# Mixer parameters first, eight halves of modulation weights beside each FFN, and the merge's weight splits on VectorE

## The chip, the cores and the metric

The kernel runs on one core of a Trainium2 chip. Its time is the device time of one execution in microseconds. The engines are named as in the profile: PE (TensorE), DVE (VectorE), ACT (ScalarE), POOL (GpSimd) and SP, the queue that issues nearly all DMAs. Each engine works through its own instruction stream in order and waits where an operand is not ready.

## The reference, cut to what matters

Two layers run over 384 tokens (128 context, 256 latent) of width 1024. Each layer is a macaron block:

```
x += 0.5 * g1 * SwiGLU1(mod(rms(x)))            # FFN 0 of the layer, inner width 2816
x += g2 * Mix(mod(rms(x)))                      # four mixers, sigmoid-gated merge, output projection
x += 0.5 * g3 * SwiGLU2(mod(rms(x)))            # FFN 1 of the layer
```

`mod` scales and shifts by modulation vectors. A layer has nine of them (mod 0 to 8); each is `cond @ w_ada[:, 1024*mod : 1024*mod+1024] + b` for two conditionings, one for context and one for latent tokens. The mixers are a gated DeltaNet (chunked, with a triangular solve), a differential attention with QK norm, rotary and a scalar lambda from `da_lambda`, an mLSTM, and a retention with learned decay. The merge computes `sum over m of sigmoid(h @ w_gate[m]) * (branch[m] @ w_branch[m])`. Everything is in float32.

## The kernel before, in words

A float32 product is made of three TensorE matmuls over operands that are split into a high and a low part (`mm3`, L185 to L187): high by high, high by low and low by high. Activations are split once. Weights are split as they arrive: SP loads a raw block of 1 MB (`raw`, three buffers), ACT casts it to `whi` (L168), and DVE or POOL subtracts, `wlo = raw - whi` (L172). `whi` and `wlo` have three buffers each. One such split of 128x1024 elements feeds 24 matmuls of 384 columns.

An FFN is a gate/up part and a down part. Gate/up takes 44 splits; after each pair comes a Silu on ACT, a product and a second split of the hidden activations (L578, L582 on DVE). The down part takes 22 splits in two groups of output columns; each group ends with residual additions into the state (`resid`, L538), squares for the next norm (L380) and POOL's scaling of the new state (L386).

Modulation vectors are computed beside the FFNs, in two ways. A job on TensorE (`ada`) loads half a weight block (`araw`, 2 x 1 MB), and runs 16 matmuls (`arow`, L261) and, once for a vector, four transposes (`acol`, L271). The way beside, `ada_beside`, does a half (512 columns) on DVE: it loads four `braw` blocks of 512 KB (two buffers), runs 16 accumulations of 128x512 (`acc`, L315 and L317), and two transposes with two reductions (L323, L324); eight tiny matmuls (L329) finish a vector. It is cut into steps of two instructions, ten for a half, and the FFN's `split` lets one step follow each weight split that DVE does. What is left when the splits are through runs at the end of the FFN.

In the mixers small parameter loads stand where they are used. In the attention mixer, SP loads `rope`, `bgn` and `blp` (the lambda vectors), DVE multiplies and reduces `blp` (L1112, L1113), and POOL builds `brg` from the norm gains and the rotary table (L1102, L1107). The DeltaNet solve is a forward substitution on DVE: 31 rows, each a product (L1335, growing from 112x1 to 112x961) and a reduction (L1337), one after the other. Beside it TensorE has the rest of the attention and work of the merge to do: gates (`mg`, one split and 24 matmuls each) and products (`pb`) with the branch weights, each finished by one DVE instruction on `y` (L1485). In the merge, the low parts of the splits for the mixers m = 3, 2 and 1 (the tuple POOLM: 24 gates and 6 branch halves a layer) are on POOL, and those of m = 0 on DVE.

The order of each engine's instructions is set when the kernel is built: a scheduler with a simulated timeline places instructions by its own costs, and what it wrote is then fixed.

Of the kernel before, what the change touches and what calls it, by code (L numbers as in the profile page):

```python
# [20 lines left out]
KD = 8  # L21
# [17 lines left out]


LOOK, NBR, LAG = 2, 8, 7
POOLM = (3, 2, 1)
EARLY = (10, 7)
EARLY0 = 6
RING, NT1, NT2 = 256 * 305, 6, 4
R_G, R_B, R_CV, R_NG, R_RT, R_N = 0, 24, 96, 114, 118, 122
# [70 lines left out]
class Trunk:  # L117
# [431 lines left out]
    def ffn_body(self, l, i, jobs, beside, nxt):  # L549
        nc, I = self.nc, self.I  # L550
        g = None
# [38 lines left out]
        for dg in range(2):  # L590
            acc = [self.mmps(name="pd") for _ in range(4)]
            units = []
            for f in range(0, KF, 4):
                nf = min(4, KF - f)
                raw = self.load_raw(
                    I["ffn_w_down"][l, i, 128 * f:128 * (f + nf), 512 * dg:512 * dg + 512].rearrange(
                        "(k p) n -> p k n", p=128), [128, nf, 512])
                for q in range(0, nf, 2):
                    w = split(raw[:, q:q + 2], [128, 2, 512])
                    units += [(f + q + r, w[0][:, r], w[1][:, r]) for r in range(2)]  # L600
                    if f + q < KF - 4:
# [113 lines left out]
    def gate_stage(self, l, keep, p):  # L715
        nc, I = self.nc, self.I
        grow = p.tile([128, T], F32, tag="grow", name="grow")
        nc.scalar.copy(grow, self.proj_gates(l))
        gb = p.tile([128, 4, 8], F32, tag="gb", name="gb")
        nc.vector.memset(gb[:, 0], 0.0)  # L720
        al = p.tile([128, 8], F32, tag="al", name="al")
        for dst, nm in ((gb[:, 1], "dn_dt_bias"), (gb[:, 2], "ml_i_bias"), (gb[:, 3], "ml_f_bias"), (al, "dn_a_log")):
            nc.sync.dma_start(dst, I[nm][l].rearrange("d h -> (d h)").unsqueeze(0).to_broadcast([128, 8]))
# [17 lines left out]
        nc.scalar.activation(out=al, in_=al, func=AF.Exp)  # L741
# [114 lines left out]

    def mix_ret(self, l, p):
        nc, I = self.nc, self.I
        lg = p.tile([128, 12], F32, name="lg")
        nc.sync.dma_start(lg[:, 0:8], I["ret_decay_logit"][l].rearrange("d h -> (d h)").unsqueeze(0).to_broadcast([128, 8]))  # L860
        nc.vector.tensor_copy(lg[:, 8:12], self.prm[l][:, R_RT:R_RT + 4])
        nc.vector.tensor_scalar_mul(lg, lg, -1.0)
        self.softplus(lg, [128, 12])
        nc.vector.tensor_scalar_mul(lg, lg, -1.0)
# [225 lines left out]

    def mix_attn(self, l, p):
        nc, I = self.nc, self.I
        lam0 = 0.8 - 0.6 * math.exp(-0.3 * l)
        rope = p.tile([128, 2, 2, 32], F32, name="rope")
        nc.sync.dma_start(rope, I["rope"])
        gn = p.tile([128, 2, 32], F32, name="bgn")
        nc.sync.dma_start(gn[:, 0], I["da_qn_g"][l:l + 1].to_broadcast([128, 32]))
        nc.sync.dma_start(gn[:, 1], I["da_kn_g"][l:l + 1].to_broadcast([128, 32]))

        rg = p.tile([128, 2, 2, 2, 32], F32, name="brg")  # L1100
        for b in range(2):
            nc.gpsimd.tensor_tensor(rg[:, b, 0], gn, rope[:, b, 0].unsqueeze(1).to_broadcast([128, 2, 32]), op=ALU.mult)  # L1102
            for a in range(2):
                sv, gv, ov = (t.rearrange("p i (g a e) -> p i g a e", a=2, e=8) for t in (
                    rope[:, b, 1].unsqueeze(1).to_broadcast([128, 2, 32]), gn, rg[:, b, 1]))
                for i in range(2):
                    nc.gpsimd.tensor_tensor(ov[:, i, :, a], gv[:, i, :, 1 - a], sv[:, i, :, a], op=ALU.mult)  # L1107
        lp = p.tmp([128, 2, 2, 32], "blp")
        nc.sync.dma_start(lp, I["da_lambda"][l].rearrange("a d -> (a d)").unsqueeze(0).to_broadcast([128, 128]).rearrange(
            "p (a b d) -> p a b d", a=2, b=2))  # L1110
        lam = p.tile([128, 2], F32, name="blam")
        nc.vector.tensor_tensor(lp[:, :, 0], lp[:, :, 0], lp[:, :, 1], op=ALU.mult)  # L1112
        nc.vector.tensor_reduce(lam, lp[:, :, 0], axis=AX, op=ALU.add)  # L1113
        nc.scalar.activation(out=lam, in_=lam, func=AF.Exp)
        nlam = p.tile([128, 1], F32, name="bnlam")
        nc.vector.scalar_tensor_tensor(nlam, lam[:, 1:2], -lam0, lam[:, 0:1], op0=ALU.add, op1=ALU.subtract)
        gcol = p.tile([128, 1], F32, name="bgc")
        nc.vector.tensor_scalar_mul(gcol, self.prm[l][:, R_NG + 1:R_NG + 2], 1.0 - lam0)
# [322 lines left out]
    def merge(self, l, br, y):  # L1441
# [2 lines left out]
        pend, cur = [], {}  # L1444

        def gate(m, d):
            eng = nc.gpsimd if m in POOLM else nc.vector
            if d % 2 == 0:
                cur["g"] = self.wcols(I["w_in"][l], C_MERGE + 1024 * m + 128 * d)
            q = d % 2  # L1450
            w = self.split_unit(cur["g"][:, :, 128 * q:128 * q + 128], [128, KD, 128], eng)
            ps = self.hidden(w, "mg")
            if m > 1 or d % 4 == 3:
                s = self.wp.tile([128, T], F32, tag="nt", name="mgs", bufs=2)
            else:
                s = self.bp.tile([128, T], F32, tag="br", name="mgs", bufs=NBR)
            with self.tc.high_priority():
                nc.scalar.activation(out=s, in_=ps, func=AF.Tanh, scale=0.5)
            pend.append((m, d, s))

        def prepare(m, d):
            eng = nc.gpsimd if m in POOLM else nc.vector
# [32 lines left out]
        for t in range(n):  # L1495
# [6 lines left out]
            for i, u in enumerate(due):  # L1502
# [62 lines left out]
    def run(self):  # L1565
        with self.es:
# [6 lines left out]
            for l in range(2):  # L1573
                if l:
                    self.norm()
                else:
                    with self.after(self.last_load):
                        self.nc.sync.dma_start(self.cst[:, NC1:], self.I["cst2"])
                mods = {(0, 0): (0, (2, 3, 4)), (0, 1): (0, (8,)), (1, 0): (1, (3, 4)), (1, 1): None}
                slow = {(0, 0): ((0, 5), (0, 6), (0, 7)), (0, 1): ((1, 0), (1, 1), (1, 2)), (1, 0): ((1, 5), (1, 6), (1, 7)),  # L1580
                        (1, 1): ((1, 8),)}
                jobs = [self.ada(mods[l, i][0], *mods[l, i][1]) if mods[l, i] else iter(()) for i in range(2)]
# [34 lines left out]
```

## Time and profile before

| | |
|---|---|
| time, median of 3 runs | 2138.11 us (2131.19 to 2139.86) |
| profiled execution | 2140.96 us, span 2139.2 us |
| mean granted TensorE clock | 0.978 |
| PE busy | 2062.1 us (96%) |
| DVE busy | 1469.3 us (69%) |
| ACT busy | 842.9 us (39%) |
| POOL busy | 466.2 us (22%) |
| read from device memory | 313.00 MB |

The stages lie in the trace at about: FFN 0 of layer 0 until 333 us, its mixers and merge until 830 us, FFN 1 until 1110 us, FFN 0 of layer 1 until 1385 us, its mixers and merge until 1870 us, and the last FFN. A time in a row is counted from the start of the span. "Idle before" is what an engine waited in front of an instruction, with what ended the wait.

### The profile page before, as it was taken

What the parts mean: (1) busy time and instruction counts of PE and PEld (TensorE: products, weight loads), DVE (VectorE), ACT (ScalarE), POOL (GpSimd) and SP (SyncE); (2) the same over time, 40 slices, a digit from 0 to 9 for tenths busy, and PEclk for the clock granted to TensorE, in tenths of its full rate; (3) what the DMA queues carried; (4) which work ended last, traced back from release to release, by engine and by line L of the source; (5) the groups of instructions that cost most, each with busy time, mean ns of one, the idle gap of its engine ahead of it and who ended that gap; (6) DMA issues with size and microseconds to landing.
All of it is one profiled execution on the core that took longest, in us unless ns stands there. A gap on an engine that the chain in (4) does not pass through costs nothing.

```text
span 2139.2 us, 31932 instructions
## 1 busy us (share of the span) xinstructions
PE 2062.1 (96%) x12450; PEld 1992.0 (93%) x12450; DVE 1469.3 (69%) x2716; ACT 842.9 (39%) x1514; POOL 466.2 (22%) x375
## 2 busy tenths in 40 slices
PE   7999999988899999999999999999888999999999
PEld 5889999888789999999999999999877999999999
DVE  4867678678955578776778776678699445795433
ACT  3533335453343245333344332363533423463322
POOL 3000014434354252000120000243243722500000
PEclk8999999999899999999999999999998999999999
DMA  9775545434142355565467554444332423454432
GB/s 312 266 266 171 172 139 173 132 97 121 52 123 70 111 187 171 185 186 178 148 221 260 169 177 168 144 127 138 99 99 77 116 72 129 148 167 128 135 123 79
DMA packets 280566, 322.75 MB, mean 151 GB/s; under 512 B 42784, under 2 KB 214368, under 8 KB 280160
## 3 DMA queue, kind: packets, MB, share of 16 engines
q1 hardware_dynamic: 280144, 320.46, 47.7%
q8 instruction: 98, 1.61, 0.3%
q14 instruction: 52, 0.43, 0.1%
q10 hardware_dynamic: 272, 0.26, 0.0%
HBM read 313.00 MB, written 7.69 MB: 150 GB/s over the span
## 4 chain that ended last, share of the span: by engine, by line
PE 83%; DVE 13%; DMA 2%; ACT 1%; issue 1%; SPq 0%; DVEq 0%; ACTq 0%
PE pg L185 6%; PE pd L185 6%; PE pg L186 6%; PE pd L186 6%; PE pd L187 6%; PE pg L187 6%; PE pu L187 6%; PE pu L185 6%; PE pu L186 6%; PE mg L187 3%; PE mg L185 3%; PE mg L186 3%; DVE aR L1335 2%; PE mm L185 1%; PE mm L186 1%; PE mx L1389 1%
## 5 line engine op out<-in xcount | busy, mean ns | idle before, releaser
L168 ACT CAST whi<-raw 128x1024 fp32r<-128x1024 f32 x422 | 442.6, 1050 | 880.8 <-PE pd L186 212.9
L172 DVE TENSOR_TENSOR wlo<-raw,whi 128x1024 fp32r<-128x1024 f32 x324 | 401.3, 1239 | 304.1 <-ACT whi L168 298.8
L172 POOL TENSOR_TENSOR wlo<-raw,whi 128x1024 fp32r<-128x1024 f32 x98 | 246.4, 2518 | 331.6 <-ACT whi L168 304.9
L386 POOL TENSOR_SCALAR xg<-xT,gs 128x128 f32<-128x128 f32 (+1 forms) x96 | 92.8, 982 | 798.3 <-DVE xT L538 775.7
L185 PE MATMUL pd<-hh,whi 128*128 128x384 f32 x704 | 237.6, 337 | 0.0
L186 PE MATMUL pd<-hl,whi 128*128 128x384 f32 x704 | 237.3, 337 | 0.0
L187 PE MATMUL pd<-hh,wlo 128*128 128x384 f32 x704 | 234.8, 337 | 0.0
L317 DVE SCALAR_TENSOR_TENSOR acc<-braw,cond,acc 128x512 f32<-128x512 f32 x280 | 198.7, 749 | 0.2 <-DMA braw<-in_w_ada 0.2
L185 PE MATMUL pg<-hhi,whi 128*128 128x384 f32 x536 | 180.2, 336 | 0.0
L186 PE MATMUL pg<-hlo,whi 128*128 128x384 f32 x536 | 179.4, 335 | 0.0
L187 PE MATMUL pg<-hhi,wlo 128*128 128x384 f32 x536 | 179.3, 334 | 0.0
L185 PE MATMUL pu<-hhi,whi 128*128 128x384 f32 x536 | 179.1, 334 | 0.0
L187 PE MATMUL pu<-hhi,wlo 128*128 128x384 f32 x536 | 179.1, 334 | 0.0
L186 PE MATMUL pu<-hlo,whi 128*128 128x384 f32 x536 | 179.1, 334 | 0.0
L185 PE MATMUL mg<-hhi,whi 128*128 128x384 f32 x512 | 178.0, 348 | 0.0
L186 PE MATMUL mg<-hlo,whi 128*128 128x384 f32 x512 | 177.3, 346 | 0.0
L187 PE MATMUL mg<-hhi,wlo 128*128 128x384 f32 x512 | 175.5, 344 | 0.9 <-DVE wlo L172 0.9
L186 PEld LDWEIGHTS pd<-hl,whi 128*128 128x128 f32 x704 | 132.3, 188 | 0.1
L185 PEld LDWEIGHTS pd<-hh,whi 128*128 128x128 f32 x704 | 132.3, 188 | 0.1
L187 PEld LDWEIGHTS pd<-hh,wlo 128*128 128x128 f32 x704 | 132.1, 188 | 0.0
L185 PEld LDWEIGHTS pg<-hhi,whi 128*128 128x128 f32 x536 | 100.6, 188 | 3.6 <-ACT hh L581 3.4
L186 PEld LDWEIGHTS pg<-hlo,whi 128*128 128x128 f32 x536 | 100.7, 188 | 1.7 <-issue 1.7
(417 smaller groups left out, 4629.5 us busy)
## 6 DMA issues: line engine op xcount, KB each, us to landing
raw<-in_w_in SPq DMA_DIRECT2D x62, 1024.0 KB
raw<-in_ffn_w_gate SPq DMA_DIRECT2D x44, 1024.0 KB
raw<-in_ffn_w_up SPq DMA_DIRECT2D x44, 1024.0 KB
braw<-in_w_ada SPq DMA_DIRECT2D x80, 512.0 KB
raw<-in_ffn_w_down SPq DMA_DIRECT2D x40, 1024.0 KB
araw<-in_w_ada SPq DMA_DIRECT2D x32, 1024.0 KB
raw<-in_w_branch SPq DMA_DIRECT2D x16, 512.0 KB
raw<-in_w_out SPq DMA_DIRECT2D x8, 1024.0 KB
```

What stands on the lines that cost most here:

```text
L168: nc.scalar.copy(hi, src)
L172: self.last_split = (eng or nc.vector).tensor_tensor(lo, src, hi.bitcast(F32), op=ALU.subtract)
L185: nc.tensor.matmul(ps, w[0], x[0], start=start, stop=False)
L186: nc.tensor.matmul(ps, w[0], x[1], start=False, stop=False)
L187: self.last_mm = nc.tensor.matmul(ps, w[1], x[0], start=False, stop=stop)
L317: nc.vector.scalar_tensor_tensor(acc[s], raw[:, g], c, acc[s], op0=ALU.mult, op1=ALU.add)
L386: self.nc.gpsimd.tensor_scalar(xg[kk][:, a:e], self.xT[:, kk, a:e], gs[:, s, kk:kk + 1], None, op0=ALU.mult)
L1335: nc.vector.tensor_tensor(pr, X[:, 0:r, 0:r].rearrange("p k c -> p c k"), M[:, r, 0:r].unsqueeze(1).to_broadcast([112, r, r]), op=ALU.mult)
L1389: nc.tensor.matmul(ps[:, 64 * h:64 * h + 64], Z[d][:, b, h], x[:, 64 * h:64 * h + 64], start=(h == 0), stop=(h == 3))
```

## The change

There are three parts. First, the parameter loads of the mixers and the small work on them move into `mixer_parameters`, which is written ahead of everything else in `mixers`. Second, in an FFN's down part two steps of `ada_beside` follow each split in place of one, and the vectors move: the TensorE jobs lose three (mod 4 of layer 0, mods 3 and 4 of layer 1), and the work beside grows from six halves to eight in three FFNs. Third, POOLM is gone: all gate and branch splits of the merge have their low part on DVE.

```
-POOLM = (3, 2, 1)
...
-        def split(src, shape):
+        def split(src, shape, n=1):
             w = self.split_unit(src, shape)
             if self.last_split.ins.engine == mybir.EngineType.DVE:
                 with self.after(self.last_split):
-                    next(beside, None)
+                    for _ in range(n):
+                        next(beside, None)
...
-                    w = split(raw[:, q:q + 2], [128, 2, 512])
+                    w = split(raw[:, q:q + 2], [128, 2, 512], 2)
...
         def gate(m, d):
-            eng = nc.gpsimd if m in POOLM else nc.vector
...
-            w = self.split_unit(cur["g"][:, :, 128 * q:128 * q + 128], [128, KD, 128], eng)
+            w = self.split_unit(cur["g"][:, :, 128 * q:128 * q + 128], [128, KD, 128])
...
-                cur["w"] = self.split_unit(cur["raw"].pop(0), [128, 2, 512], eng)
+                cur["w"] = self.split_unit(cur["raw"].pop(0), [128, 2, 512])
...
+    def mixer_parameters(self, l):
...
+        lp = self.ring.tmp([128, 2, 2, 32], "blp")
...
+        for dst, nm in ((self.gb[:, 1], "dn_dt_bias"), (self.gb[:, 2], "ml_i_bias"), (self.gb[:, 3], "ml_f_bias"),
+                        (self.al, "dn_a_log"), (self.lg[:, 0:8], "ret_decay_logit")):
+            nc.sync.dma_start(dst, I[nm][l].rearrange("d h -> (d h)").unsqueeze(0).to_broadcast([128, 8]))
+        nc.sync.dma_start(lp, I["da_lambda"][l].rearrange("a d -> (a d)").unsqueeze(0).to_broadcast([128, 128]).rearrange(
+            "p (a b d) -> p a b d", a=2, b=2))
...
     def mixers(self, l):
         nc = self.nc
         with self.pool("bp") as self.bp:
+            self.mixer_parameters(l)
...
-                mods = {(0, 0): (0, (2, 3, 4)), (0, 1): (0, (8,)), (1, 0): (1, (3, 4)), (1, 1): None}
-                slow = {(0, 0): ((0, 5), (0, 6), (0, 7)), (0, 1): ((1, 0), (1, 1), (1, 2)), (1, 0): ((1, 5), (1, 6), (1, 7)),
-                        (1, 1): ((1, 8),)}
+                mods = {(0, 0): (0, (2, 3)), (0, 1): (0, (8,))}
+                slow = {(0, 0): ((0, m) for m in (4, 5, 6, 7)), (0, 1): ((1, m) for m in (0, 1, 2, 3)),
+                        (1, 0): ((1, m) for m in (4, 5, 6, 7)), (1, 1): ((1, 8),)}
```

The rows below are instructions in the order that the builds give an engine, with the line, the operation, out<-in and the shape. The lines of the changed kernel are its own.

VectorE near the end of the down part of the first FFN, before (`wlo` is a weight split, `acc` the work beside, the memsets belong to the mixers):

```order
L172 TENSOR_TENSOR wlo<-raw,whi 128x1024
L317 SCALAR_TENSOR_TENSOR acc<-braw,cond,acc 128x512 x2
L720 MEMSET gb 128x8
L172 TENSOR_TENSOR wlo<-raw,whi 128x1024
L317 SCALAR_TENSOR_TENSOR acc<-braw,cond,acc 128x512 x2
L647 MEMSET raw 128x1024
L791 MEMSET mp 36x3
L784 MEMSET m_3220 36x1
L172 TENSOR_TENSOR wlo<-raw,whi 128x1024
L317 SCALAR_TENSOR_TENSOR acc<-braw,cond,acc 128x512 x2
```

The same place in the changed kernel:

```order
L171 TENSOR_TENSOR wlo<-raw,whi 128x1024
L316 SCALAR_TENSOR_TENSOR acc<-braw,cond,acc 128x512 x2
L171 TENSOR_TENSOR wlo<-raw,whi 128x1024
L316 SCALAR_TENSOR_TENSOR acc<-braw,cond,acc 128x512 x2
L800 COPY mp<-m_3307 4x1 x2
L316 SCALAR_TENSOR_TENSOR acc<-braw,cond,acc 128x512 x2
L171 TENSOR_TENSOR wlo<-raw,whi 128x1024
L316 SCALAR_TENSOR_TENSOR acc<-braw,cond,acc 128x512 x4
L322 STREAM_TRANSPOSE acct<-acc 128x512
L171 TENSOR_TENSOR wlo<-raw,whi 128x1024
```

Two accumulations follow a split before; now most splits have four behind them, and the work beside runs until the last split.

VectorE in the later half of the substitution of layer 0, before (`aR` is the substitution; `bmx`, `brc`, `bsum`, `be` the attention's softmax; `y` a product of the merge):

```order
L1335 TENSOR_TENSOR aR<-aR 112x529
L1184 TENSOR_SCALAR bmx<-bmx 128x2
L1337 TENSOR_REDUCE aR<-aR 112x23
L1335 TENSOR_TENSOR aR<-aR 112x576
L1193 RECIPROCAL brc<-bsum 128x2
L1337 TENSOR_REDUCE aR<-aR 112x24
L1194 SCALAR_TENSOR_TENSOR bsum<-brc,bnlam,bsum 128x1
L1335 TENSOR_TENSOR aR<-aR 112x625
L1195 SCALAR_TENSOR_TENSOR be<-be,bsum 128x384
L1337 TENSOR_REDUCE aR<-aR 112x25
L1335 TENSOR_TENSOR aR<-aR 112x676
L1485 SCALAR_TENSOR_TENSOR y<-mgs,pb 128x384
```

The same place in the changed kernel:

```order
L1300 TENSOR_TENSOR aR<-aR 112x484
L171 TENSOR_TENSOR wlo<-raw,whi 128x1024
L1448 SCALAR_TENSOR_TENSOR y<-mgs,pb 128x384
L1302 TENSOR_REDUCE aR<-aR 112x22
L1158 RECIPROCAL brc<-bsum 128x2
L1300 TENSOR_TENSOR aR<-aR 112x529
L1159 SCALAR_TENSOR_TENSOR bsum<-brc,blam,bsum 128x1
L1302 TENSOR_REDUCE aR<-aR 112x23
L1160 SCALAR_TENSOR_TENSOR be<-be,bsum 128x384
L1300 TENSOR_TENSOR aR<-aR 112x576
L171 TENSOR_TENSOR wlo<-raw,whi 128x1024
L1448 SCALAR_TENSOR_TENSOR y<-mgs,pb 128x384
```

The splits now stand between the rows of the substitution: 11 between its first and its last product, where there was none, and 10 merge products there in place of 7.

VectorE where `blp` was multiplied, in the attention mixer of layer 0, before (`fr` and `nu` are steps of an inverse square root, `co` an output of the retention or mLSTM):

```order
L161 SCALAR_TENSOR_TENSOR fr<-nu,fr 128x12
L159 SCALAR_TENSOR_TENSOR nu<-fr 128x12
L160 TENSOR_TENSOR nu<-nu,nv 128x12
L1112 TENSOR_TENSOR blp<-blp 128x2x32
L161 SCALAR_TENSOR_TENSOR fr<-nu,fr 128x12
L666 TENSOR_TENSOR co<-co,fr 128x256 x3
L172 TENSOR_TENSOR wlo<-raw,whi 128x1024
```

Where it stands in the changed kernel, at the start of the first FFN of layer 0:

```order
L171 TENSOR_TENSOR wlo<-raw,whi 128x1024
L316 SCALAR_TENSOR_TENSOR acc<-braw,cond,acc 128x512 x2
L578 TENSOR_TENSOR sg<-sg,hn 128x384 x2
L271 TENSOR_REDUCE sb<-acol 128x4
L1497 TENSOR_TENSOR blp<-blp 128x2x32
L209 TENSOR_TENSOR hn<-pg,sqacc 128x384
L209 TENSOR_TENSOR hn<-pu,sqacc 128x384
L582 TENSOR_TENSOR hl<-sg,hh 128x384 x2
```

The scheduler moved the layer 0 instance ahead of the mixers by a whole FFN, with its load right behind the load of a raw gate block; that of layer 1 went into the merge of layer 0.

## Rows read from the trace of the kernel before

**Rows 1.** The page: busy time by engine, and the chain that ended last by engine.

```profile
PE 2062.1 (96%) x12450; PEld 1992.0 (93%) x12450; DVE 1469.3 (69%) x2716; ACT 842.9 (39%) x1514; POOL 466.2 (22%) x375
...
PE 83%; DVE 13%; DMA 2%; ACT 1%; issue 1%; SPq 0%; DVEq 0%; ACTq 0%
```

**Rows 2.** Windows: us, busy (instructions) of five engines, PE clock, DMA share, GB/s.

```profile
100.00:200.00 100.00, 100.00 (x604) 92.90 (x603) 68.05 (x102) 35.37 (x53) 0.00 (x0) 1.00 0.73 237
```

**Rows 3.** Timeline of PE around modulation work: start us, us, instruction, count.

```profile
160.41 0.60 PE L271 MATMUL acol<-cst,mrow 128*128 128x128 f32 x4
...
165.30 0.26 PE L329 MATMUL mx<-xa,cst 128*32 128x16 f32 x8
...
1169.97 1.93 PE L261 MATMUL arow<-araw,cond 128*32 128x512 f32 x16
1171.82 0.44 PE L185 MATMUL pg<-hhi,whi 128*128 128x384 f32 x1
```

**Rows 4.** Timeline of DVE in the down part of the first FFN.

```profile
258.67 1.23 DVE L172 TENSOR_TENSOR wlo<-raw,whi 128x1024 fp32r<-128x1024 f32 x1 [1.61 <-ACT whi L168]
259.81 1.41 DVE L317 SCALAR_TENSOR_TENSOR acc<-braw,cond,acc 128x512 f32<-128x512 f32 x2
262.83 1.22 DVE L172 TENSOR_TENSOR wlo<-raw,whi 128x1024 fp32r<-128x1024 f32 x1 [1.61 <-ACT whi L168]
```

**Rows 5.** Window over the 22 down splits of the first FFN.

```profile
221.00:312.50 91.50, 91.50 (x535) 91.21 (x534) 65.16 (x93) 29.82 (x39) 7.68 (x11) 1.00 0.50 161
```

**Rows 6.** Groups of DVE instructions: count, busy us, mean ns, idle before, releasers.

```profile
L317 DVE SCALAR_TENSOR_TENSOR acc<-braw,cond,acc 128x512 f32<-128x512 f32 x280 | 198.7, 749 | 0.2 <-DMA braw<-in_w_ada 0.2
```

**Rows 7.** Chain that ended last, at the start: a 512 KB load.

```profile
1.63 4.13 DMA xr<-in_x_prompt
```

**Rows 8.** Chain that ended last, around `blp` in both layers.

```profile
476.82 8.14 DMA blp<-in_da_lambda
```
```profile
1517.46 8.36 DMA blp<-in_da_lambda
```

**Rows 9.** Timeline of PE behind these waits, with idle before.

```profile
485.88 0.69 PE L673 MATMUL mx<-cst,co 128*128 128x128 f32 x2 [10.83 <-DVE co L666]
```
```profile
1527.99 0.58 PE L640 MATMUL mm<-wlo,hhi 128*128 128x256 f32 x1 [7.05 <-DVE wlo L172]
```

**Rows 10.** Windows behind these waits, columns as in Rows 2.

```profile
480.00:490.00 10.00, 4.12 (x20) 4.13 (x20) 4.91 (x11) 0.59 (x1) 1.65 (x2) 0.50 0.59 150
...
1520.00:1530.00 10.00, 2.95 (x16) 2.74 (x15) 4.05 (x13) 2.17 (x4) 1.52 (x1) 0.80 0.52 130
```

**Rows 11.** Timeline of POOL during the substitution of layer 0.

```profile
541.07 2.38 POOL L172 TENSOR_TENSOR wlo<-raw,whi 128x1024 fp32r<-128x1024 f32 x1 [7.08 <-ACT whi L168]
...
583.34 6.09 POOL L172 TENSOR_TENSOR wlo<-raw,whi 128x1024 fp32r<-128x1024 f32 x2 [8.38 <-ACT whi L168]
```

**Rows 12.** Timeline of DVE during the same substitution.

```profile
540.73 0.38 DVE L1335 TENSOR_TENSOR aR<-aR 112x121 f32<-112x121 f32 x1
541.15 0.28 DVE L1337 TENSOR_REDUCE aR<-aR 112x11 f32<-112x121 f32 x1
541.46 2.18 DVE L1335 TENSOR_TENSOR aR<-aR 112x144 f32<-112x144 f32 x1
...
550.30 0.21 DVE L1194 SCALAR_TENSOR_TENSOR bsum<-brc,bnlam,bsum 128x1 f32<-128x1 f32 x1
...
584.82 2.29 DVE L1194 SCALAR_TENSOR_TENSOR bsum<-brc,bnlam,bsum 128x1 f32<-128x1 f32 x1
```

**Rows 13.** Page: the groups of weight splits on DVE and on POOL.

```profile
L172 DVE TENSOR_TENSOR wlo<-raw,whi 128x1024 fp32r<-128x1024 f32 x324 | 401.3, 1239 | 304.1 <-ACT whi L168 298.8
L172 POOL TENSOR_TENSOR wlo<-raw,whi 128x1024 fp32r<-128x1024 f32 x98 | 246.4, 2518 | 331.6 <-ACT whi L168 304.9
```

**Rows 14.** Window over that substitution, columns as in Rows 2.

```profile
530.00:590.00 60.00, 49.19 (x249) 42.84 (x248) 59.04 (x100) 20.56 (x47) 22.36 (x8) 0.89 0.25 71
```

**Rows 15.** Timeline of SP and of DVE at the start of the first FFN.

```profile
75.66 0.37 SPq L177 DMA_DIRECT2D raw<-in_ffn_w_gate  x1
```
```profile
80.50 0.17 DVE L272 TENSOR_REDUCE sb<-acol 128x4 f32<-128x16 f32 x1
```

More of the change, by code (lines that the diff above doesn't have):

```diff
@@ L718, in gate_stage @@
         nc.scalar.copy(grow, self.proj_gates(l))
[L719 to L723, printed above, removed]
+        gb, al = self.gb, self.al
         tp = self.mxps([128, 3, 128])
@@ L740, in gate_stage @@
         self.softplus(sp.rearrange("p b a r -> p (b a r)"), [128, 48])
-        nc.scalar.activation(out=al, in_=al, func=AF.Exp)
         nc.vector.scalar_tensor_tensor(sp[:, :, 0], sp[:, :, 0], -1.0, al.unsqueeze(1).to_broadcast([128, 3, 8]),
@@ L858, in mix_ret @@
         nc, I = self.nc, self.I
[L859 to L864, printed above, removed]
+        lg = self.lg
         dm = p.tile([128, 2, 4, 128], F32, name="dm")
@@ L1092, in mix_attn @@
         nc, I = self.nc, self.I
[L1093 to L1118, printed above, removed]
+        gn, rg, nlam, gcol = self.gn, self.rg, self.nlam, self.gcol
         xt = p.tile([128, 3, 2, 256], F32, name="bx")
@@ L1461, in prepare @@
         def prepare(m, d):
-            eng = nc.gpsimd if m in POOLM else nc.vector
             if d == 0:
@@ L1507, in merge @@
                 product(*pend[u])
+    def mixer_parameters(self, l):
+        nc, I, bp = self.nc, self.I, self.bp
+        lam0 = 0.8 - 0.6 * math.exp(-0.3 * l)
+        self.gb = bp.tile([128, 4, 8], F32, name="gb", bufs=1)
+        self.al = bp.tile([128, 8], F32, name="al", bufs=1)
+        self.lg = bp.tile([128, 12], F32, name="lg", bufs=1)
+        lp = self.ring.tmp([128, 2, 2, 32], "blp")
+        lam = bp.tile([128, 4], F32, name="blam", bufs=1)
+        rope = self.ring.tmp([128, 2, 2, 32], "rope")
+        self.gn = bp.tile([128, 2, 32], F32, name="bgn", bufs=1)
+        nc.vector.memset(self.gb[:, 0], 0.0)
+        for dst, nm in ((self.gb[:, 1], "dn_dt_bias"), (self.gb[:, 2], "ml_i_bias"), (self.gb[:, 3], "ml_f_bias"),
[3 more added lines that the diff above has]
+            "p (a b d) -> p a b d", a=2, b=2))
+        nc.sync.dma_start(self.gn[:, 0], I["da_qn_g"][l:l + 1].to_broadcast([128, 32]))
+        nc.sync.dma_start(self.gn[:, 1], I["da_kn_g"][l:l + 1].to_broadcast([128, 32]))
+        nc.sync.dma_start(rope, I["rope"])
+        nc.scalar.activation(out=self.al, in_=self.al, func=AF.Exp)
+        nc.vector.tensor_copy(self.lg[:, 8:12], self.prm[l][:, R_RT:R_RT + 4])
+        nc.vector.tensor_scalar_mul(self.lg, self.lg, -1.0)
+        self.softplus(self.lg, [128, 12])
+        nc.vector.tensor_scalar_mul(self.lg, self.lg, -1.0)
+        nc.vector.tensor_tensor(lp[:, :, 0], lp[:, :, 0], lp[:, :, 1], op=ALU.mult)
+        nc.vector.tensor_reduce(lam[:, 0:2], lp[:, :, 0], axis=AX, op=ALU.add)
+        nc.scalar.activation(out=lam[:, 0:2], in_=lam[:, 0:2], func=AF.Exp)
+        self.nlam, self.gcol = lam[:, 2:3], lam[:, 3:4]
+        nc.vector.scalar_tensor_tensor(self.nlam, lam[:, 1:2], -lam0, lam[:, 0:1], op0=ALU.add, op1=ALU.subtract)
+        nc.vector.tensor_scalar_mul(self.gcol, self.prm[l][:, R_NG + 1:R_NG + 2], 1.0 - lam0)
+        self.rg = rg = bp.tile([128, 2, 2, 2, 32], F32, name="brg", bufs=1)
+        for b in range(2):
+            nc.gpsimd.tensor_tensor(rg[:, b, 0], self.gn, rope[:, b, 0].unsqueeze(1).to_broadcast([128, 2, 32]), op=ALU.mult)
+            for a in range(2):
+                sv, gv, ov = (t.rearrange("p i (g a e) -> p i g a e", a=2, e=8) for t in (
+                    rope[:, b, 1].unsqueeze(1).to_broadcast([128, 2, 32]), self.gn, rg[:, b, 1]))
+                for i in range(2):
+                    nc.gpsimd.tensor_tensor(ov[:, i, :, a], gv[:, i, :, 1 - a], sv[:, i, :, a], op=ALU.mult)
@@ L1578, in run @@
                         self.nc.sync.dma_start(self.cst[:, NC1:], self.I["cst2"])
-                mods = {(0, 0): (0, (2, 3, 4)), (0, 1): (0, (8,)), (1, 0): (1, (3, 4)), (1, 1): None}
-                slow = {(0, 0): ((0, 5), (0, 6), (0, 7)), (0, 1): ((1, 0), (1, 1), (1, 2)), (1, 0): ((1, 5), (1, 6), (1, 7)),
-                        (1, 1): ((1, 8),)}
-                jobs = [self.ada(mods[l, i][0], *mods[l, i][1]) if mods[l, i] else iter(()) for i in range(2)]
+                mods = {(0, 0): (0, (2, 3)), (0, 1): (0, (8,))}
+                slow = {(0, 0): ((0, m) for m in (4, 5, 6, 7)), (0, 1): ((1, m) for m in (0, 1, 2, 3)),
+                        (1, 0): ((1, m) for m in (4, 5, 6, 7)), (1, 1): ((1, 8),)}
+                jobs = [self.ada(mods[l, i][0], *mods[l, i][1]) if (l, i) in mods else iter(()) for i in range(2)]
                 beside = [self.ada_beside([(*m, hf) for m in slow[l, i] for hf in range(2)]) for i in range(2)]
```

## The prediction

> **What bounds the kernel now.** I read the page first: PE is busy for 2062.1 us of 2139.2, and the chain that ended last is 83% PE and 13% DVE [rows 1]. So two things count: instructions taken off PE where it is full, and stretches where PE waits. The windows by stage come next. In the FFNs PE is busy without a gap at full clock, with DVE at about two thirds [rows 2]; there only fewer matmuls help, and more DVE work is free until DVE is full. The missing 77 us lie at the start and in the mixers. Two stretches there belong to this change. In both layers the chain passes through the load of `blp`, 8.14 and 8.36 us [rows 8], behind which PE sat idle for 10.83 and 7.05 us [rows 9], with a lower clock around it: 0.50 in the window after the first wait, 0.80 in that of the second [rows 10]. And during the substitution DVE is busy for 59.04 of 60 us and PE for 49.19, at a clock of 0.89 [rows 14]: DVE sets the pace of that stage.
>
> **Vectors taken off PE.** For one half of a vector the 16 `arow` matmuls take 1.85 us from their start to the next matmul's start, 1.93 as listed; the four `acol` transposes last 0.60, once a vector [rows 3]. A vector is two halves: 2 x 1.85 + 0.60 = 4.3 us. Beside, it gives back the eight tiny matmuls, 0.26 [rows 3]. Net 4.0 us, three vectors: **-12 us**. These stand in FFNs where PE has no gap, so all of it should show.
>
> **The work beside, doubled in the down parts.** Each of three FFNs gets two halves more, 20 steps, and by the order all 20 fall behind down splits. A step is two accumulations, 1.41 us as listed [rows 4], so 28.2 us of DVE work. The first FFN's down part is the tightest: in its 91.5 us DVE is busy for 65.16 [rows 5], and 26.3 are free, nearly all as the 1.61 us in front of each split [rows 4]. So DVE would come to 93.4 of 91.5 us by listed times; by starts it is less, since a split listed with 1.23 us lets the next instruction begin after 1.14 [rows 4]. The cover (DVE's idle time) is thus just used up. In a period of 4.16 us (262.83 less 258.67) a split and four accumulations need 1.14 + 2.8 = 3.9, and residuals, squares and the last transposes must pass too. Three `wlo` buffers let DVE fall behind by a split or so before PE notices. I take +2 us for each FFN, **+6 us**; the low end is 0, the high end is the third rival.
>
> The rows show one more load on DVE: POOL is busy for 7.68 us in that part [rows 5], and a DVE instruction that meets a POOL one can be held (below). The Trainium skill, page "SBUF — State Buffer", section "Who interferes with whom", says that a DVE instruction with two SBUF inputs and a GpSimd instruction that reads SBUF share a read port, which is locked for the whole instruction, so that the second one waits. Both the split and the accumulation have two inputs in SBUF. By that rule up to 7.68 us a part come on top of a DVE that is already full; it is the fourth rival.
>
> **The `blp` waits.** DVE multiplied `blp` in front of work that PE waited for. Without the load, layer 0's idle time of 10.83 us shrinks to what DVE needs for three `co` instructions and PE's own hand-over; I leave 1.5, so -9.3. In layer 1 the releaser was a split behind `blp` in DVE's queue; freed of 8.36 us it is ready before PE runs dry, so -7.0. The clock: at 0.50 over 4.12 busy us and 0.80 over 2.95 [rows 10] some 2 + 0.6 us were lost, and as much again in the slices behind; I count 2.5. Together **-19 us**; bounds -23 (all the idle time and clock) and -8 (another wait takes half of it).
>
> **Where these loads go.** By the order, layer 0's `blp` stands at DVE right behind the `sb` that ran at 80.50, and its load behind the raw gate load issued at 75.66 [rows 15]. If it lands as slowly as in the mixers, 8.14 us [rows 8], DVE waits to about 84: some 4 us, of which the buffers ahead of PE hide about half. At the start of each mixer stage SP now issues nine small loads together, in front of `al` and `lg` work on ACT and DVE. The cover is the splits made ahead. I take **+3 us** in all; bounds 0 and +16 (second rival).
>
> **The merge's splits.** During the substitution POOL did seven of them, from 541.07 to 583.34 [rows 11]. Five DVE instructions beside them were stretched, from 541.46 (2.18 us, its smaller neighbour 0.38) to 584.82 (2.29, its like 0.21) [rows 12]: each lasts until POOL's split ends, and together they are some 9.8 us longer than their neighbours. The reduction at 541.15 beside the same POOL split kept its 0.28 [rows 12]. Now 11 splits of 1.14 us and three products more, about 0.5 each, stand on DVE: 12.5 + 1.6 - 9.8 = 4.3 us longer. In exchange PE gets four gates more in that stretch, each 24 matmuls at 100 us / 604 [rows 2], 4.0 us, and three products of 1 us: 19 us of work that need not follow later, against 10.8 us of idle time there and about 6.6 lost to the clock [rows 14]. If half of the idle time fills, the layer gains 5. Both layers: **-10 us**. The bounds are +4 a layer (DVE's extra time alone) and -17 (idle time and clock together). After the substitution a split costs 1239 ns on DVE in place of 2518 on POOL [rows 13], so low parts come earlier, and DVE has room.
>
> The shared port explains the stretch: by the skill's rule just named the stretched instructions have two SBUF inputs and the reduction has one, and the rows agree. It says nothing about the gain on PE, since the time it frees is spent on the splits.
>
> **Sum.** -12 + 6 - 19 + 3 - 10 = -32. From the profiled execution, 2140.96, that is 2109; from the median of the runs, 2.85 lower, 2106. I take 2108.
>
> **Rivals.**
> First: DVE becomes a longer chain in the merge. A split on DVE waits for ACT's cast, and everything queued behind it, the next row of the substitution first, waits too; on POOL only POOL waited. The order puts splits directly in front of rows, and DVE was full already [rows 14]. Then the merge costs +4 a layer in place of -5: 2108 + 18 = 2126. Against it: casts are made ahead, and POOL's own stretch was as large.
> Second: the parameter waits move rather than go. If DVE's wait at 80 us costs PE its full 8, and each mixer start 4, the +3 becomes +16 and with a residual of 3 at the old places: 2124. For it: the load is slow wherever it stood [rows 8]; against: DVE reaches it late enough in layer 1.
> Third, the slow side: the down parts become bound by `braw`. A load of 512 KB took 4.13 us from issue to landing on an empty queue [rows 7]; a buffer is in use for 2.8 us by two steps. Behind a raw block of 1 MB, about 3 us more, a cycle of two buffers takes 2.8 + 4.1 + 3 = 9.9, or 5.0 a split against the 4.16 of PE. Over 22 splits that is 18 us an FFN, and 54 for three in place of 6: 2156. It decides from the point where DVE waits for `braw` in most periods. For it: the buffers stay two while the rate doubles. Against it: the only such wait now is 0.2 us [rows 6], and DMA is busy half of the time [rows 5].
> Fourth, from the port: POOL's 7.68 us come on top of DVE's 93.4 in each down part; PE waits 9.6 in place of 2, 2108 + 23 = 2131. Against it: the 65.16 already hold the stretched instructions of that part.
> That the change does not move what it says is excluded by the order.
>
> **How the numbers follow.** Forecast 0.50 (its own range 2096 to 2120), first rival 0.17, second 0.12, third 0.13, fourth 0.08. About what a measurement can tell from no change is 0.5%, 10.7 us: 2127.4 and 2148.8. Faster: the forecast, most of the second, half of the first and a little of the fourth, 0.72. Same: the rest of these, 0.14. Slower: the third and a little more, 0.14. The range goes from 2094 (merge and waits at their better ends) to 2142, which leaves out the third rival and few others.
>
> **What would show it.** PE without `arow` for mod 4 in the first FFN and for mods 3 and 4 in the third; the down parts still 91 to 94 us long with DVE above 95% and no wait for `braw` above 1 us each; no DVE wait for `blp` in the mixers, and one of a few us at about 80 us; in the substitution no DVE instruction of 112x144 above 1 us, PE busy above 90%. The prediction is wrong if the down parts grow by more than 5 us each, or if the stretch from the first to the last row of the substitution grows by more than 8 us without PE being fuller.

## The result, and the profile after

The changed kernel takes 2103.57 us (median of 4 runs, 2103.37 to 2104.16), the kernel before 2137.02 beside it: a ratio of 0.9848, 95% interval 0.9834 to 0.9861, or some 33 us less. The forecast was 2108.

The page of the changed kernel, busy time and chain, which answers to [rows 1]:

```profile
PE 2038.8 (97%) x12366; PEld 1976.7 (94%) x12366; DVE 1561.3 (74%) x2893; ACT 840.9 (40%) x1511; POOL 320.2 (15%) x315
...
PE 82%; DVE 13%; DMA 2%; issue 2%; ACT 1%; SPq 0%; DVEq 0%; ACTq 0%
```

The span fell by 36.8 us, from 2139.2 to 2102.4. PE is busy for 23.3 us less and idle for 13.5 less. About 12 us of the first are, by the prediction's price, the three vectors (the page counts 84 PE instructions less); the rest goes with a higher granted clock, 0.987 in place of 0.978 over the span. With the merge splits alone (below), where PE has the 12450 instructions of before, it is busy for 2048.1 us in place of 2062.1, at 0.986.

The next table cuts the two stages of mixers by the first matmul of three kinds in the trace: `mm` (input projections), `mg` (merge gates) and `pg` (the next FFN's gate). Each entry is the difference of two start times, in us; "front" is from `mm` to `mg`, "merge" from `mg` to `pg` and holds the substitution. The kernels below the second row are those of the experiments. Each row is one execution, and the profiled one of before, 2140.96 us, is longer than that kernel's other undisturbed runs (2130.5 to 2139.9). The merge of layer 0 reads 288.3 before and 284.4 with the vectors alone, which do not touch it; the fronts of the changed kernel and of the two with added POOL work in the merge are up to 1.7 us apart. So some 4 us between two merges, or 2 between two fronts, say nothing.

| kernel | front, layer 0 | merge, layer 0 | front, layer 1 | merge, layer 1 |
|---|---|---|---|---|
| before | 190.6 | 288.3 | 184.6 | 287.4 |
| changed | 187.9 | 274.0 | 188.8 | 274.0 |
| parameters alone | 177.2 | 291.2 | 186.2 | 290.6 |
| vectors alone | 189.5 | 284.4 | 185.2 | 287.1 |
| merge splits alone | 183.6 | 274.1 | 184.4 | 272.7 |
| parameters alone, lg chain back | 177.9 | 285.9 | 176.8 | 289.5 |
| changed, lg chain back | 185.1 | 273.3 | 179.9 | 274.8 |
| changed, lg chain back, projections on DVE | 168.4 | 279.7 | 171.8 | 284.1 |
| changed, projections on DVE | 168.8 | 273.0 | 173.2 | 283.0 |
| changed, lg chain back, no split on POOL | 174.9 | 279.9 | 172.2 | 283.9 |
| changed, added POOL reads | 187.8 | 290.6 | 187.1 | 296.5 |
| changed, added POOL writes | 186.3 | 272.8 | 188.1 | 274.3 |

So the merge gave 14 us in each layer, and the front, where the `blp` waits were, nearly nothing. The FFNs gave the rest: the third lost 8.5 us (1094.0 to 1381.6 before, 1074.9 to 1354.0 now), which is about what two vectors were priced at.

**The down parts.** DVE in the first FFN, timeline and then a window over PE's whole down part, against [rows 4] (the window of [rows 5] covers another stretch, so the same stretch of before stands here too). The changed kernel:

```profile
260.19 1.23 DVE L171 TENSOR_TENSOR wlo<-raw,whi 128x1024 fp32r<-128x1024 f32 x1 [0.23 <-ACT whi L167]
261.33 2.73 DVE L316 SCALAR_TENSOR_TENSOR acc<-braw,cond,acc 128x512 f32<-128x512 f32 x4
264.35 1.23 DVE L171 TENSOR_TENSOR wlo<-raw,whi 128x1024 fp32r<-128x1024 f32 x1 [0.29 <-ACT whi L167]
```
```profile
237.90:330.40 92.50, 92.50 (x547) 91.93 (x547) 86.09 (x134) 28.78 (x36) 15.39 (x19) 1.00 0.67 207
```
The kernel before:
```profile
240.50:332.60 92.10, 92.10 (x543) 91.56 (x544) 64.37 (x98) 30.68 (x39) 13.41 (x19) 1.00 0.53 163
```

The period is still 4.16 us; the idle time ahead of a split went from 1.61 to some 0.26, and PE has no gap. The part is 0.4 us longer, the other two 0.4 each. The group of accumulations, against [rows 6], waits a little for `braw` now, 2.6 us in all:

```profile
L316 DVE SCALAR_TENSOR_TENSOR acc<-braw,cond,acc 128x512 f32<-128x512 f32 x364 | 257.0, 747 | 2.8 <-DMA braw<-in_w_ada 2.6
```

**The substitution.** The window of [rows 14] in the changed kernel, and its groups of splits, against [rows 13]:

```profile
530.00:590.00 60.00, 57.43 (x318) 51.75 (x316) 57.73 (x113) 25.52 (x59) 2.93 (x1) 0.94 0.30 88
```
```profile
L171 DVE TENSOR_TENSOR wlo<-raw,whi 128x1024 fp32r<-128x1024 f32 x384 | 476.8, 1242 | 272.0 <-ACT whi L167 266.8
...
L171 POOL TENSOR_TENSOR wlo<-raw,whi 128x1024 fp32r<-128x1024 f32 x38 | 94.3, 2482 | 128.9 <-ACT whi L167 102.1
```

DVE is about as full as before, yet PE is busy for 57.43 us in place of 49.19, at a clock of 0.94 in place of 0.89. The first and the last product of the substitution, before and then in the changed kernel:

```profile
534.47 0.15 DVE L1335 TENSOR_TENSOR aR<-aR 112x1 f32<-112x1 f32 x1
...
593.85 1.79 DVE L1335 TENSOR_TENSOR aR<-aR 112x961 f32<-112x961 f32 x1
```
```profile
529.30 0.15 DVE L1300 TENSOR_TENSOR aR<-aR 112x1 f32<-112x1 f32 x1
...
594.54 1.97 DVE L1300 TENSOR_TENSOR aR<-aR 112x961 f32<-112x961 f32 x1
```

**The front.** PE's idle times there, against [rows 9], in the changed kernel:

```profile
374.36 0.84 PE L743 MATMUL mx<-sp,cst 128*128 128x24 f32 x3 [6.27 <-DVE sp L739]
...
477.12 0.69 PE L673 MATMUL mx<-cst,co 128*128 128x128 f32 x2 [3.98 <-DVE co L666]
...
1405.23 1.05 PE L743 MATMUL mx<-sp,cst 128*128 128x24 f32 x4 [4.27 <-DVE sp L739]
```

The stop of 10.83 us shrank to 3.98, that of 7.05 is gone, and two new ones stand at the gate chain (`sp`), where PE did not stop before. The early `blp` waited for its load only briefly, for 2.02 us, and PE stayed busy for 10.00 of the 10 us from 80 to 90:

```profile
84.67 0.23 DVE L1497 TENSOR_TENSOR blp<-blp 128x64 f32<-128x64 f32 x1 [2.02 <-DMA blp<-in_da_lambda]
```

### The profile page after: what moved, and what is told of

Its sections match the earlier page's. It is cut to its first block, busy times and chain, and to the rows that moved or that the text cites. A ratio compares the mean times of both kernels' runs of the same rounds, so it can differ in the third digit from the quotient of the medians.

```text
span 2102.4 us, 31907 instructions
## 1 busy us (share of the span) xinstructions
PE 2038.8 (97%) x12366; PEld 1976.7 (94%) x12366; DVE 1561.3 (74%) x2893; ACT 840.9 (40%) x1511; POOL 320.2 (15%) x315
## 4 chain that ended last, share of the span: by engine, by line
PE 82%; DVE 13%; DMA 2%; issue 2%; ACT 1%; SPq 0%; DVEq 0%; ACTq 0%
PE pg L184 6%; PE pg L185 6%; PE pg L186 6%; PE pu L184 6%; PE pu L186 6%; PE pu L185 6%; PE pd L184 6%; PE pd L185 6%; PE pd L186 6%; PE mg L185 3%; PE mg L184 3%; PE mg L186 3%; DVE wlo L171 2%; PE mx L1354 1%; DVE aR L1300 1%
## 5 line engine op out<-in xcount | busy, mean ns | idle before, releaser
L171 DVE TENSOR_TENSOR wlo<-raw,whi 128x1024 fp32r<-128x1024 f32 x384 | 476.8, 1242 | 272.0 <-ACT whi L167 266.8
L316 DVE SCALAR_TENSOR_TENSOR acc<-braw,cond,acc 128x512 f32<-128x512 f32 x364 | 257.0, 747 | 2.8 <-DMA braw<-in_w_ada 2.6
L1450 POOL TENSOR_TENSOR y<-y,mgs 128x384 f32<-128x384 f32 x48 | 62.7, 1318 | 433.1 <-DVE mgs L1448 415.6
L171 POOL TENSOR_TENSOR wlo<-raw,whi 128x1024 fp32r<-128x1024 f32 x38 | 94.3, 2482 | 128.9 <-ACT whi L167 102.1
L186 PEld LDWEIGHTS mg<-hhi,wlo 128*128 128x128 f32 x512 | 97.3, 190 | 8.5 <-DVE wlo L171 8.0
```

Of the source, the lines that this page charges most:

```text
L171: self.last_split = (eng or nc.vector).tensor_tensor(lo, src, hi.bitcast(F32), op=ALU.subtract)
L186: self.last_mm = nc.tensor.matmul(ps, w[1], x[0], start=False, stop=stop)
L316: nc.vector.scalar_tensor_tensor(acc[s], raw[:, g], c, acc[s], op0=ALU.mult, op1=ALU.add)
L1450: nc.gpsimd.tensor_tensor(y[:, d], y[:, d], s, op=ALU.add)
```

## The experiments

### One part at a time

```
parameters alone:   the kernel before + mixer_parameters(l) first in mixers
vectors alone:      the kernel before + the new mods and slow, and split(..., 2) in the down part
merge splits alone: the kernel before with
-POOLM = (3, 2, 1)
+POOLM = ()
```

> The kernel before with the first part alone: parameters first, modulation vectors and merge splits as before. Theory (the prediction's terms): -19 for the waits on blp and +3 elsewhere, so about 2121 us. Rival, from the trace of the changed kernel, where the mixers up to the first gate of the merge are only 2.7 us shorter in layer 0 and 4.2 us longer in layer 1: the idle time moves to the stop in front of the matmuls on sp (6.27 and 4.27 us there), and little is won: 2131 to 2138 us.

Measured 2136.1 us, ratio to before 1.0003 (0.9992 to 1.0014): nothing. The rival's number holds, its place does not: in this trace PE has no stop in front of `sp`. In layer 0 the front is 13.4 us shorter, in layer 1 it is 1.6 longer, and the merge reads 3 more in each, which is within what the table can tell. So where the 13 us went is shown only in part.

> The kernel before with the second part alone: eight halves beside three FFNs, two steps behind each down split, three vectors off PE. Prediction's terms: -12 + 6 = -6, about 2131 us. Theory from the trace after (down parts 92.2, 92.3, 92.1 us before and 92.3, 92.5, 92.4 after): -12 + 1, about 2126 us. Rival (down parts bound by braw): above 2150 us.

Measured 2128.02 us, 0.9969 (0.9958 to 0.9981), -4 to -9 us: the prediction's term, -12 + 6. The down parts take 92.5 us or so against 92.1, as in the changed kernel; the rival is out.

> The kernel before with the third part alone: all merge splits on DVE. Prediction's term: -10, about 2127 us. Theory from the trace after (first gate of the merge to the first output projection 254.1 and 253.1 us before, 239.6 and 239.5 after): -28, about 2109 us, with PE over 90% busy in the substitution. Rival (a longer DVE chain): 2145 us.

Measured 2105.6 us, 0.986 (0.984 to 0.9879): -30 us, three times the prediction's term. The three parts by themselves sum to -36; together they gave -33. All that the change gained lies in the second and the third part.

### Where in the merge

```
-            w = self.split_unit(cur["g"][...], [128, KD, 128])
+            w = self.split_unit(cur["g"][...], [128, KD, 128], nc.gpsimd if m in POOLM else nc.vector)
             (prepare likewise; POOLM = (2, 1), and POOLM = (3,))
```

> The changed kernel with the merge splits of m = 2 and 1 on POOL again, m = 3 on DVE. The gates of m = 3 and a few of m = 2 run beside the substitution, the others behind it. Theory (the gain lies in the substitution): half or more of the 28 us stays, 2105 to 2117 us. Rival (the gain lies behind the substitution, where a split's low part comes 1.3 us sooner): 2120 us and more.

Measured 2107.56 us, 0.9877 (0.9857 to 0.9897).

> The changed kernel with the merge splits of m = 3 on POOL again, m = 2 and 1 on DVE. Theory (the gain lies in the substitution): 2115 us or more. Rival (it lies behind it): 2104 to 2110 us.

Measured 2124.51 us, 0.995 (0.9931 to 0.9968). POOL splits for m = 3 cost 21 us, and of these ten a layer 7 and 6 ran beside the substitution; those of m = 2 and 1 cost 4 to 6, and of these twenty a layer 5 and 4 ran beside it. The theory that the gain lies in the substitution holds in the main: 15 or 16 splits a layer behind it and a few beside it cost little.

### Is it the order, or POOL's access?

Here the order of DVE and of PE is the changed kernel's, instruction by instruction; only POOL does more, on half a raw block behind its last reader:

```
+            if m > 1 and q == 0:
+                t = cur["g"][:, :, 0:128]
+                with self.after(self.last_split):
+                    for _ in range(2):          # the other kernel: range(5), memset(t, 0.0)
+                        nc.gpsimd.tensor_tensor(t, t, self.cst[:, 0:1024].rearrange("p (k n) -> p k n", k=KD), op=ALU.mult)
             ps = self.hidden(w, "mg")
```

> The changed kernel, with two more POOL instructions of the split's size (128x1024, two inputs in SBUF) behind every second gate split of m = 3 and 2; they overwrite a raw block that nobody reads any more, and DVE and PE have the same order as in the changed kernel. Theory (a POOL instruction that reads SBUF holds up DVE instructions with two SBUF inputs): some five pairs beside each substitution stretch it by 2 to 4 us each, together +12 to +35 us, 2116 to 2138 us. Rival (POOL's work beside DVE costs nothing, the gain came from the order alone): within 3 us of 2103.6.

Measured 2136.68 us, 1.0016 (1.0006 to 1.0027): the whole gain of the change is gone.

> As the kernel with added POOL instructions that read, but POOL only writes: five memsets of 128x1024 behind every second gate split of m = 3 and 2. Theory (only POOL instructions that read SBUF hold DVE up): within 3 us of 2103.6. Rival (any POOL access holds DVE up): as long as the kernel whose POOL instructions read.

Measured 2099.95 us, 0.9842 (0.9827 to 0.9858): no loss. The two differ by 37 us, and by the table it lies in the merges (290.6 and 296.5 us against 272.8 and 274.3). The same substitution rows in both, first where POOL reads (timelines of POOL and DVE):

```profile
551.92 5.72 POOL L1420 TENSOR_TENSOR raw<-raw,cst 128x1024 f32<-128x1024 f32 x2 [14.41 <-DVE wlo L171]
```
```profile
549.62 0.56 DVE L1300 TENSOR_TENSOR aR<-aR 112x225 f32<-112x225 f32 x1
...
555.77 2.27 DVE L1300 TENSOR_TENSOR aR<-aR 112x256 f32<-112x256 f32 x1
558.07 0.42 DVE L1302 TENSOR_REDUCE aR<-aR 112x16 f32<-112x256 f32 x1
```
and where it only writes:
```profile
543.96 5.01 POOL L1420 MEMSET raw<- 128x1024 f32 x5 [10.51 <-DVE wlo L171]
```
```profile
541.69 0.55 DVE L1300 TENSOR_TENSOR aR<-aR 112x225 f32<-112x225 f32 x1
...
546.63 0.64 DVE L1300 TENSOR_TENSOR aR<-aR 112x256 f32<-112x256 f32 x1
547.18 0.80 DVE L1149 TENSOR_SCALAR bmx<-bmx 128x2 f32<-128x2 f32 x1
```

The row 112x256 takes 2.27 us in the one, ending 0.4 us behind POOL's instruction (557.64), and 0.64 in the other in the middle of five memsets. So it is over the whole trace. Of 35 DVE instructions TENSOR_TENSOR or SCALAR_TENSOR_TENSOR that began while an added instruction of POOL ran, 23 were more than 0.2 us longer than their like elsewhere where POOL reads, some 40 us together; where it only writes it is none of 66. Windows of 60 us from 532 on, POOL about equally busy; where it reads and where it writes:

```profile
532.00:592.00 60.00, 52.24 (x271) 46.21 (x270) 59.28 (x104) 21.76 (x51) 21.90 (x8) 0.89 0.24 73
```
```profile
532.00:592.00 60.00, 56.92 (x321) 51.58 (x320) 59.30 (x108) 24.72 (x53) 25.78 (x24) 0.97 0.32 96
```

DVE looks full in both. PE falls from 56.92 to 52.24 and its clock from 0.97 to 0.89, as in [rows 14]. The Trainium skill, page "SBUF — State Buffer", section "Who interferes with whom", says that only a GpSimd instruction that reads SBUF contends with a DVE instruction of two SBUF inputs, not one that only writes; these two kernels agree, 2.27 us against 0.64. The pair shows that reads of POOL beside the merge can cost as much as the change gained. It does not show that all of the 30 us of the merge splits came from there, for a low part also comes earlier when DVE makes it; the 4 to 6 us for m = 2 and 1 suggest that this is the small part.

### Why the front gained nothing

The part of `mixer_parameters` that works on `lg`, the retention's decay (three DVE instructions and a softplus, 20 dependent DVE steps in all), is moved back; the loads stay first.

```
     def mix_ret(self, l, p):
         lg = self.lg
+        nc.vector.tensor_copy(self.lg[:, 8:12], self.prm[l][:, R_RT:R_RT + 4])
+        nc.vector.tensor_scalar_mul(self.lg, self.lg, -1.0)
+        self.softplus(self.lg, [128, 12])
+        nc.vector.tensor_scalar_mul(self.lg, self.lg, -1.0)
     (and taken out of mixer_parameters)
```

> The changed kernel, with the loads still first but the retention's decay chain (four DVE instructions and a softplus on lg) moved back to where the retention mixer starts. Theory: the early lg lets POOL begin the decay matrices (dm, rqx) 10 us sooner, beside the gate chain of DVE, whose small instructions are stretched from 0.2 to 0.65 us and more, and PE, which has 233 matmuls before sp in place of 269, runs dry. Then the stops of 6.27 and 4.27 us go: 2092 to 2096 us. Rival: the stops come from PE's order alone, however lg is placed: 2101 to 2105 us.

Measured 2093.23 us, 0.9804 (0.9789 to 0.982): by the ratios 9 us better than the changed kernel. The stops at `sp` shrink from 6.27 and 4.27 us to 1.70 and 1.38.

> The kernel before with the first part alone, except that the retention's decay chain on lg stays where the retention mixer starts. Theory: the first part gained nothing by itself because the early chain on lg delayed the norm and the gate chain by about what the blp waits gave; without it the gain shows: ratio to the kernel before 0.992 to 0.996 (some 2119 to 2127 us by its median). Rival: the blp waits were no gain in any order (PE's idle time only spreads): 0.998 to 1.002.

Measured 2121.67 us, 0.9932 (0.9915 to 0.9949): the first part does gain 11 to 18 us over the kernel before, once the chain on `lg` stays behind. Beside the other two parts it gains less: the vectors alone (0.9969) and the merge splits alone (0.986) make 0.983 together, and the changed kernel with the chain back stands at 0.9804, some 5 us lower, which the intervals do not set apart from nothing. The rows show two ways in which the early chain cost. In layer 0 it let POOL begin the decay matrices (`dm`) and what hangs on them (`rqx`) while DVE was in the gate chain; POOL and DVE in the changed kernel:

```profile
364.64 2.14 POOL L859 TENSOR_TENSOR dm<-dm,cst 128x512 f32<-128x512 f32 x2
...
367.69 2.77 POOL L888 TENSOR_TENSOR rqx<-rqT,qd 128x256 f32<-128x256 f32 x4
```
```profile
367.84 0.65 DVE L694 TENSOR_TENSOR lz<-lz,se 128x48 f32<-128x48 f32 x1
368.52 0.65 DVE L695 TENSOR_TENSOR lq<-lz 128x48 f32<-128x48 f32 x1
```
and DVE with the chain moved back, where two such instructions (one of them smaller) take 0.27:
```profile
365.16 0.27 DVE L694 TENSOR_TENSOR lz<-lz,se 128x48 f32<-128x48 f32 x2
```

In layer 1 the chain was woven into the norm's inverse square root, and POOL's projection splits held both up. POOL and DVE in the changed kernel, the last row being the end of that root:

```profile
1364.42 2.37 POOL L171 TENSOR_TENSOR wlo<-raw,whi 128x1024 fp32r<-128x1024 f32 x1
```
```profile
1364.49 2.32 DVE L158 SCALAR_TENSOR_TENSOR nu<-nr 128x3 f32<-128x3 f32 x1
...
1367.04 0.16 DVE L160 SCALAR_TENSOR_TENSOR nr<-nu,nr 128x3 f32<-128x3 f32 x1
```
with the chain moved back:
```profile
1360.15 0.16 DVE L160 SCALAR_TENSOR_TENSOR nr<-nu,nr 128x3 f32<-128x3 f32 x1
```

The root ends 13.0 us after the first `mm` in the one (1367.04 less 1354.0) and 9.5 in the other (1360.15 less 1350.7). That is 3.5 of the 8.9 us by which the front of layer 1 differs; the `sp` stop is another 3. In layer 0 the early chain cost the front 2.8 us (187.9 against 185.1), little more than the table can tell, and nothing in the kernels with the parameters alone (177.2 against 177.9). So the `lg` chain does not explain why layer 0's front is 8 us longer in the changed kernel with the chain back than with the parameters alone; that stays open, but for POOL's part in it, which follows.

### POOL's other splits

In the mixers' projections every second split is still on POOL. Both kernels below put them on DVE; ten splits behind the norms stay on POOL.

```
     def lo_eng(self, m):
-        return self.nc.gpsimd if m else self.nc.vector
+        return self.nc.vector
```

With the chain on `lg` moved back:

> The changed kernel with the chain on lg moved back (2093.2 us), and also the weight splits of the mixers' input projections on DVE in place of every second on POOL; 10 of POOL's 38 splits are left. Theory (a POOL split costs DVE more by holding it up than the 1.14 us that DVE needs for it): 2080 to 2090 us. Rival (DVE is busy for 80% at the mixers' start, so what it takes over delays the chains there): 2094 to 2102 us.

Measured 2082.01 us, 0.975 (0.9735 to 0.9764). With the chain early, as in the changed kernel:

> The changed kernel (lg chain early, as it was) with the weight splits of the mixers' input projections on DVE; it differs from the 2082 us kernel only in the place of the lg chain. Theory: what the early chain cost was mostly POOL's splits and decay matrices holding DVE up; with most of POOL's splits gone it costs 0 to 4 us, 2082 to 2086 us. Rival: the chain's 20 dependent instructions delay the norm by themselves: 10 us as before, 2090 to 2094 us.

Measured 2075.74 us, 0.9722 (0.9706 to 0.9738): the fastest kernel here, 59 us or 2.8% below the kernel before (2135.02 us beside it). Without POOL's splits the early chain costs the front 0.4 and 1.4 us (table), where it cost 2.8 and 8.9 with them; so what it cost layer 1 went with POOL's splits, and the place of the chain by itself cost little. The 6 us by which this kernel is faster than its sister lie mostly in layer 0's merge (273.0 against 279.7); why is not shown.

The last ten splits on DVE too:

```
-        if self.units in (2, 3):
-            eng = nc.gpsimd
```

> The 2082 us kernel with the last ten POOL splits (the second and third behind each norm) on DVE too. Theory (a POOL split holds DVE up by more than DVE's 1.14 us): 2076 to 2081 us. Rival (behind a norm DVE works on the norm's chain, where its own split in the queue costs as much): 2081 to 2088 us.

Measured 2108.74 us, 0.9876 (0.9857 to 0.9895): 27 us worse than with them on POOL. Theory and rival both missed the size. DVE behind the norm ahead of the third FFN, first and last steps of the root and what stands between:

```profile
1084.16 0.16 DVE L154 TENSOR_SCALAR nv<-mx 128x3 f32<-128x3 f32 x1 [0.40 <-PE mx L425]
1084.24 1.22 DVE L169 TENSOR_TENSOR wlo<-raw,whi 128x1024 fp32r<-128x1024 f32 x1
1085.37 1.41 DVE L314 SCALAR_TENSOR_TENSOR acc<-braw,cond,acc 128x512 f32<-128x512 f32 x2
1086.69 0.17 DVE L155 TENSOR_SCALAR nr<-nv 128x3 int32<-128x3 int32 x1
...
1094.86 0.16 DVE L160 SCALAR_TENSOR_TENSOR nr<-nu,nr 128x3 f32<-128x3 f32 x1
```
and the same root in the 2076 us kernel, its second and its last step:
```profile
1058.61 2.17 DVE L155 TENSOR_SCALAR nr<-nv 128x3 int32<-128x3 int32 x1
...
1061.79 0.16 DVE L160 SCALAR_TENSOR_TENSOR nr<-nu,nr 128x3 f32<-128x3 f32 x1
```

Here a split of POOL held the second step, for 2.17 us in place of 0.17:
```profile
1058.18 2.58 POOL L171 TENSOR_TENSOR wlo<-raw,whi 128x1024 fp32r<-128x1024 f32 x1
```
Yet from the second step on, the root takes 3.3 us here and 8.3 with no split on POOL, where splits and accumulations stand between its eight small dependent steps. PE waited for it there:
```profile
1095.08 0.90 PE L430 MATMUL mx<-cst,nr 128*128 128x128 f32 x3 [5.43 <-DVE nr L160]
```

Against the 2082 us kernel the start times place nearly all of the 27 us behind four norms: 6.5 in layer 0's front (table), 2.9, 10.8 and 6.4 in the gate/up parts of the second, third and last FFN (190.3, 186.8 and 186.1 us with POOL's ten splits, 193.2, 197.6 and 192.5 without). Layer 1's front, behind the fifth, grew by 0.4. In the third FFN's first 60 us PE is busy for 51.81 us at a clock of 0.91, against 59.44 at 1.00.

## Why the prediction was right, and where it was not

The direction, the time and the range held, and so did the mechanism of the vectors and of the merge. But the closeness of the total, -33 where -32 was forecast, is luck: the parameters were priced at -16 and gave nothing, the merge at -10 and gave -30, and these two misses nearly cancelled.

- **Vectors, -12.** Right. The third FFN lost 8.5 us for two vectors, as priced. The first shows 2.1 only against the kernel before; but with merge splits alone, where nothing in it was changed, that FFN took 316.2 us (19.2 to 335.4) against 313.3 before, so the profiled execution of before was some 3 us short there.
- **Work beside, +6.** Too dear: the down parts grew by 0.4 us each. DVE came to 86.09 us of 92.5, not 93.4 of 91.5. The step that was over-counted is "A step is two accumulations": ten steps of a half hold 16 accumulations, so 20 steps are 32 accumulations and four steps of transposes and reductions, and the trace has 64 accumulations in that part where it had 32. DVE's busy time in it rose by 21.7 us (86.09 less 64.37), not by 28.2. By the runs the second part gave only -4 to -9, though, as with the +6; what took back a few us outside the down parts is not shown.
- **`blp`, -19.** This step failed. The waits for `blp` went as said, but the gain did not follow: the parameters alone gave 1.0003. "Freed of 8.36 us it is ready before PE runs dry" looked at one stop, and not at what moving twenty dependent DVE steps to the start of the stage does there. The bound of -8 ("another wait takes half of it") was too narrow. Of the rivals the second had the right idea and the wrong carrier: the waits moved, in layer 1 not with a load but with the `lg` chain and POOL; for layer 0 the carrier stays open. With that chain left in place the same step gives 11 to 18 us over the kernel before, about what was priced (-19 + 3); beside the merge splits on DVE it gives some 5, not clear of noise, so the terms do not add.
- **Merge, -10.** Right in mechanism, mis-sized by a factor of three: -30 alone, near the bound of -17 a layer. "If half of the idle time fills" was the choice that failed. In the window nearly all of it filled (10.8 us idle before, 2.6 now) and the clock recovered from 0.89 to 0.94; the substitution, from the start of its first product to that of its last, became 5.9 us longer (534.47 to 593.85 before, 529.30 to 594.54 now), 4.3 were priced. At most 2 or 3 us a layer come from the splits behind it (the kernel with m = 2 and 1 on POOL), for which the sum had no term. The first rival is out: the splits in the chain did lengthen it, and it did not matter.
- **POOL beside the down part.** The fourth rival did not come: POOL was busy for 15.39 us there, DVE for 86.09, and PE had no gap. But POOL's reads do count elsewhere: added ones cost 37 us in the pair of kernels above.
- **`braw`.** The third rival is out: 2.6 us of waiting in all.

## What to carry to other kernels

Work moved from POOL to DVE is not priced by DVE's busy time: an instruction of POOL that reads SBUF can hold one of DVE until it ends (2.3 us beside a split here), and DVE is listed as busy meanwhile, so a chain on DVE may get shorter, or PE beside it fuller, although DVE takes on more. When work is moved to the start of a stage, look at every chain that already runs there, and test the removal of a wait by itself: one part here gained nothing and hid in a good total. Splits put into a queue with a chain of tiny dependent steps are another matter; there the slow engine beside it was the better place, by 27 us here.

## What was not expected of the hardware

Not only instructions with two large inputs are held: a DVE instruction of 128x1 with small operands took 2.29 us in place of 0.21 [rows 12], one of 128x3 took 2.32 beside a POOL split, and a TENSOR_SCALAR of 128x3, which reads a single tensor, 2.17. A reduction beside a POOL split kept its length (0.28 us, [rows 12]). Beside POOL's memsets the products and accumulations kept theirs, but four of six TENSOR_SCALAR did not: the `bmx` of 128x2 shown above took 0.80 us there, 0.16 away from POOL. And a load of only 64 KB, broadcast over the partitions, took 8.14 us from its issue to its landing [rows 8], twice the 4.13 of a 512 KB load [rows 7]; other transfers had been issued just ahead of both, so how much of it is the load's own is not shown.
